# A hybrid decoder step on one core: when the pooling weights and the samples' caches are loaded

## The chip, the core and the metric

The kernel runs on one core of one Trainium2 chip. It is one launch that computes a whole layer for a prompt of 2048 tokens and for 8 samples of 8 tokens. The metric is the device time of that launch in microseconds; the smaller the better. The kernel is written with Tile, which turns the Python program into one instruction list per engine: it computes which instruction waits for which, and a list scheduler may move an instruction ahead of others of the same engine. Tiles come from fixed rings of slots, and the order in which slots are taken and given back is the order of the Python program.

## The reference

All weights are float32. `x` is the prompt or the samples, `D_MODEL` is 1024.

```python
h = rmsnorm(x, g_mix)
proj = h @ w_in                      # 512 q, 128 k, 128 v, 512 u
# 1a. window attention: 8 heads of 64, 2 kv heads, window 128, sink, ALiBi
#     prompt: blocks of 128;  samples: keys = cat(cache_win_k, k), values = cat(cache_win_v, v)
# 1b. pooling mixer on u: means over windows 2, 4, 8, 16 minus u, per channel group g
full = cat([u_prev, u])              # u_prev: state_pool for the samples, zeros for the prompt
y = einsum('blgc,gce->blge', d, w_pool) * pool_scale
x = x + cat([attn, y]) @ w_out
# 2. cross attention, 4 heads of 256, 256 memory tokens
q = rmsnorm(x, g_cross) @ w_cq;  mem_k = hm @ w_ck;  mem_v = hm @ w_cv   # hm = rmsnorm(mem)
x = x + softmax(q mem_k / 16) mem_v @ w_co
# 3. MLP
x = x + square(relu(rmsnorm(x, g_ffn) @ w_up)) @ w_down
# outputs also: the last 128 k and v rows and the last 15 u rows of prompt and samples, mem_k, mem_v
```

## The kernel before

**Arithmetic.** Every dense product is made of three TensorE matmuls: each operand is split into a high part (a float32r cast, `hi`) and the rest (`lo`), and hi·hi, hi·lo and lo·hi are added in PSUM (`mm3`, lines 122 to 124, and `dense`, lines 291 to 293). A weight chunk of 512 KB is loaded by SyncE (`SP`) into one of six float32 slots `f`, cast by ScalarE (line 143) and subtracted by VectorE (line 144) into two of twelve slots `w`; then the slot `f` is free again. `Stream` holds the list of all chunks in the order of their use and runs up to five chunks ahead, as long as enough slots are free (`pump`).

**Order of the program.** A prologue works on the prompt's memory; three superblocks of two token blocks each follow. In the prologue `mem_k` and `mem_v` are made first (chunks `wck`, `wcv`). Then comes the *query fold*, the loop over eight chunks `wcqt`: each gives two products of 128x512 that ScalarE copies from PSUM into a slot `f` (`put_fold`, line 342) and SP stores to the scratch tensor `a_s` (line 344). The *output fold* does the same with eight chunks `wco`, two at a time, into `b_s`. So in both folds the six slots `f` serve the loads and the stores. The norms of superblock 0's two blocks (`norm1`) run beside these folds.

**The lead of superblock 0.** The projection `h @ w_in` has ten chunks of 128 columns (`win`), each multiplied with block 0 (256 columns) and block 1 (320 columns, the last 64 of them the samples). A list `lead` says which products come before the attention starts: (chunk 0, block 0), (0, 1), (1, 0), (1, 1), (2, 0), (2, 1) and on to (5, 1). After each of the first four of them stands one `fold(g, wpr)`: the rows of `w_out` for pool group g (chunk `wop`) times the pooling weights, already scaled by `pool_scale` and split (`wpr`, one slot `w`), two products of 128x512 that are stored to `wo_s`. `prep_fold` makes `wpr`: it loads the constants `cst` (line 349) and the pooling weights `wpool` (line 351, 256 KB), and four ScalarE and four VectorE instructions scale and split them (lines 354, 355).

**What the samples need.** The samples' cached keys `ckz` (1 MB, line 534, into the tile X1 that held block 1's input), their cached values `cvz` (two loads of 512 KB into two slots `f`, line 522) and their pool state `spool` (line 517). `attn_sample` uses them after the lead: scores from `ckz` at line 785, values from `cvz` at line 824. The shifted caches are stored again: `out_wks` from `ckz` (line 561), `out_wvs` from `cvz` (line 778).

**Queues.** All these transfers are issued by SP, one after the other: while one of them waits for its slot, those behind it wait too.

Of the kernel before, what the change touches and what calls it, by code (L numbers as in the profile page):

```python
# [14 lines left out]
P = 128  # L15
# [41 lines left out]
def kernel(ctx: ExitStack, tc: tile.TileContext, io, nW=12, nF=6, nT=8):  # L57
    nc = tc.nc
# [288 lines left out]
    def prep_fold():  # L347
        wpr = WS.get()
        nc.sync.dma_start(cst[:], io["cst"])
        wp = FS.get()  # L350
        nc.sync.dma_start(wp[:, 0:512], io["wpool"])
        for g in range(4):
            c, sc = slice(P * g, P * g + P), vec[:, V_PSC + g:V_PSC + g + 1]
            nc.scalar.activation(wpr[:, c], wp[:, c], AF.Copy, scale=sc)
            nc.vector.scalar_tensor_tensor(wpr[:, 512 + P * g:640 + P * g], wp[:, c], sc, f32(wpr[:, c]), ALU.mult, ALU.subtract)
        FS.put(wp)
        return wpr

    def fold(g, wpr):
        th, tl = S.next(("wop", g))  # L360
        for eh in range(2):
            ps = MM.get()
            mm3(ps[:], [0], lambda k: wpr[:, P * g:P * g + P], lambda k: wpr[:, 512 + P * g:512 + P * g + P],
                lambda k: th[:, 512 * eh:512 * eh + 512], lambda k: tl[:, 512 * eh:512 * eh + 512])
            put_fold(ps[:], lambda o: [(wo_s[4 * eh:4 * eh + 4, :, P * g:P * g + P].rearrange("e p c -> p e c"),
                                        o[:, 0:512].rearrange("p (e c) -> p e c", c=P))])
            MM.put(ps)
        WS.put(th, tl)
        if g == 3:
            WS.put(wpr)  # L370

    def prologue():
        S.resW, S.resF = 1, 0
        mx = [XT[1][:, 0:1024], XT[1][:, 1024:2048]]
        mem = lambda k: mx[k // 4][:, 256 * (k % 4):256 * (k % 4 + 1)]
        warm = AUX.get()
        for _ in range(14):
            nc.tensor.matmul(warm[:, 0:P], ones[:], ident[:], start=True, stop=True)
        AUX.put(warm)
# [24 lines left out]
        pend, outs = [], []  # L404
        for name, dst in (("ck", io["mk"]), ("cv", io["mv"])):
            a = Act(256, GQ[len(outs)])
            outs.append(a)
            for c in range(8):
                th, tl = S.next((name, c))
                ps = MM.get()  # L410
                mm3(ps[:, 0:256], range(8), lambda k: w8(th)[:, k, :], lambda k: w8(tl)[:, k, :], hm.hi, hm.lo)
                WS.put(th, tl)
                pend.append((a, dst, c, ps))
                if name == "ck" and c == FINC:
                    nm.fin()
                if name == "cv" or c >= FINC:
                    while pend:
                        evac(*pend.pop(0))
                flush()
                if (name, c) == N1C:  # L420
                    norm1(blk[0][0], N1W)
        TS.put(nm.r)
        hm.free()
        mk, mv = outs
        norm1(blk[0][1], N1Q)
        for c in range(8):
            th, tl = S.next(("cq", c))
            for hf in range(2):
                ps = MM.get()
                for h2 in range(2):  # L430
                    ks = [(hf * 2 + h2) * 2, (hf * 2 + h2) * 2 + 1]
                    mm3(ps[:, 256 * h2:256 * h2 + 256], ks, lambda k: w8(th)[:, k, :], lambda k: w8(tl)[:, k, :], mk.hi, mk.lo)
                put_fold(ps[:], lambda o: [(a_s[hf, c // 2, :, 512 * (c % 2):512 * (c % 2) + 512], o[:, 0:512])])
                MM.put(ps)
            WS.put(th, tl)
            flush()
        mk.free()
        for h in range(4):
            w = [S.next(("co", 2 * h)), S.next(("co", 2 * h + 1))]
# [12 lines left out]
        mv.free()  # L452
# [46 lines left out]
    def superblock(s, blks, nxt):  # L499
        last = s == 2  # L500
        smp = blks[1] if s == 0 else None
# [12 lines left out]
        uext = X0[:, 0:4 * uw].rearrange("p (g t) -> p g t", t=uw)  # L514
        if smp:
            us = X0[:, 4 * uw:4 * uw + 736].rearrange("p (g b t) -> p g b t", g=4, t=23)
            nc.sync.dma_start(X0[:, 4 * uw:4 * uw + 736].rearrange("p (x t) -> p x t", t=23)[:, :, 0:15], io["spool"].rearrange("p (x t) -> p x t", t=15))
            ckz = X1[:, 0:2048].rearrange("p (b v s) -> p b v s", b=8, v=2)
            qz = [X1[:, 2048 + 544 * i:2048 + 544 * (i + 1)] for i in range(2)]
            cvs = [FS.get(), FS.get()]  # L520
            for i in range(2):
                nc.sync.dma_start(cvs[i][:, 0:1024], io["cvz"][:, 1024 * i:1024 * (i + 1)])
            cvz = [c[:, 0:1024].rearrange("p (b v s) -> p b v s", b=4, v=2) for c in cvs]
            smt = TS.get()
            kS = smt[:, 0:128].rearrange("p (v t) -> p v t", t=64)
            vS = smt[:, 128:384].rearrange("p (v t) -> p v t", t=P)
            nc.gpsimd.memset(smt[:, 0:384], 0.0)
            qf = TS.get()

        def in_evac(c, b, ps):  # L530
            bl = blks[b]
            n = bl.n
            if smp and (c, b) == (0, 0):
                nc.sync.dma_start(X1[:, 0:2048], io["ckz"])
                nc.gpsimd.memset(X1[:, 2048:3136], 0.0)
            if c == 0:
                for kv in range(2):
                    r = slice(64 * kv, 64 * kv + 64)
# [15 lines left out]
                if smp is bl:  # L554
                    t = TS.get()
                    nc.vector.tensor_copy(t[:, P:192], ps[:, bl.np:n])
                    nc.sync.dma_start(io["wks"][:, :, 120:128], t[:, P:192].rearrange("p (b t) -> p b t", t=8))
                    for kv in range(2):
                        r = slice(64 * kv, 64 * kv + 64)
                        nc.gpsimd.tensor_copy(kS[r, kv, :], t[r, P:192])  # L560
                        nc.sync.dma_start(io["wks"][r, :, 0:120], ckz[r, :, kv, 8:P])
                    TS.put(t)
            elif c == 1:
                nc.vector.tensor_copy(v32[:, bl.off:bl.off + n], ps[:, 0:n])
# [196 lines left out]

        def attn_sample():
            bl = smp
            LS = FS.get()
            t = st.get()
            dsm = cst[:, C_DS:C_DS + 384].rearrange("p (g s) -> p g s", s=192)
# [83 lines left out]
        def evac_in(c, b, ps):  # L850
# [2 lines left out]

        ug = dense([("in", s, c) for c in CIN], blks, hi1, lo1, evac_in, piece=2,
                   seq=lead + rest + [(c, b) for c in range(6, 10) for b in (0, 1)])
        if s == 0:
            wpr = prep_fold()
        while len(qdone) < len(lead):
            m = len(qdone)
            while len(qdone) == m:  # L860
                next(ug)
            if s == 0 and m < 4:
                fold(m, wpr)
        S.resW = RW

        def attn():
# [415 lines left out]
        down(7)  # L1282

    vcarry = [None]
    blk = [make_blks(s) for s in range(3)]
    prologue()
    for s in range(3):
# [132 lines left out]
```

## Time and profile before

| | us |
|---|---|
| median of 3 runs | 2657.72 (2656.19 to 2660.29) |
| the profiled execution, its own time | 2660.15 |
| span of the profiled execution | 2658.3 |
| TensorE (PE) busy | 2576.7 (97%) |
| VectorE (DVE) busy | 1298.3 (49%) |
| ScalarE (ACT) busy | 974.8 (37%) |
| GpSimd (POOL) busy | 658.9 (25%) |

The profile gives the busy time of each engine, the clock that TensorE was granted, and for each instruction its start, its duration and, where its engine stood idle before it, how long and which instruction ended that idle time (the releaser). PE is the row of matmuls, PEld that of weight loads. `f<-in_win` means that a slot `f` is written from the input tensor `win`. An SP row is the issue of a transfer and not the transfer; its duration is the time the issue took. Matmuls overlap, so the distance of two starts, not the duration, says how fast they follow each other.

### The profile page before, as it was taken

Reading aid. Unit: us, or ns where it says so; the run is one execution under the profiler, and the core shown is the slowest. Engines: PE = TensorE matmul, PEld = TensorE weight load, DVE = VectorE, ACT = ScalarE, POOL = GpSimd, SP = SyncE. Lnnn points to the kernel's source line nnn. Section 1 sums busy time; section 2 is a strip of 40 time slices with the busy share of each in tenths; the row PEclk is TensorE's granted clock in tenths of the full one; section 3 lists DMA queues with packets and bytes.
Section 4 is the critical chain, followed back from the end, with each engine's and each line's share of the span. In section 5 each row is a group of like instructions: output and inputs, shape, how many; then the busy total and the mean of one; then the engine's idle time right before and its main releaser. Section 6 shows DMA issues by size and latency. Waiting matters only on the chain.

```text
span 2658.3 us, 36411 instructions
## 1 busy us (share of the span) xinstructions
PE 2576.7 (97%) x14409; PEld 2407.6 (91%) x14409; DVE 1298.3 (49%) x2256; ACT 974.8 (37%) x1867; POOL 658.9 (25%) x695
## 2 busy tenths in 40 slices
PE   8789999999999999999999999999999999999998
PEld 8688858888879998899999999999979999999997
DVE  7547634644447856353333333689363633333333
ACT  6536424422334744333222222358243422222221
POOL 1205312311125343142111111525332411111111
PEclk9989999999999999999999999999999999999999
DMA  8842266223233041212111111222211111111101
GB/s 275 265 149 89 104 238 237 79 93 104 95 102 128 25 145 33 74 45 72 64 56 64 56 64 56 81 107 81 97 48 64 56 64 64 56 64 56 64 24 50
DMA packets 101823, 245.10 MB, mean 92 GB/s; under 512 B 21972, under 2 KB 41876, under 8 KB 101012
## 3 DMA queue, kind: packets, MB, share of 16 engines
q1 hardware_dynamic: 101652, 242.78, 26.9%
q8 instruction: 113, 1.85, 0.3%
q14 instruction: 58, 0.48, 0.1%
HBM read 219.79 MB, written 22.95 MB: 91 GB/s over the span
## 4 chain that ended last, share of the span: by engine, by line
PE 80%; DVE 8%; ACT 4%; POOL 3%; DMA 3%; issue 2%; SPq 0%; DVEq 0%; ACTq 0%; POOLq 0%
PE mm L124 13%; PE mm L122 13%; PE mm L123 13%; PE mm L292 13%; PE mm L293 12%; PE mm L291 12%; DVE t L243 3%; DVE w L144 1%; POOL t L217 1%; ACT w L143 1%; PE aux L699 1%; DVE acth L246 1%; POOL t L617 1%; ACT x L711 1%; PE aux L730 1%
## 5 line engine op out<-in xcount | busy, mean ns | idle before, releaser
L143 ACT CAST w<-f 128x1024 fp32r<-128x1024 f32 x311 | 325.9, 1050 | 693.3 <-PE mm L123 470.0
L144 DVE TENSOR_TENSOR w<-f,w 128x1024 fp32r<-128x1024 f32 x311 | 393.3, 1269 | 302.8 <-ACT w L143 298.4
L291 PE MATMUL mm<-acth,w 128*128 128x400 f32 (+3 forms) x1568 | 532.6, 340 | 6.6 <-ACT w L143 5.9
L293 PE MATMUL mm<-acth,w 128*128 128x400 f32 (+3 forms) x1568 | 529.4, 338 | 1.2 <-DVE w L144 1.2
L292 PE MATMUL mm<-acth,w 128*128 128x400 f32 (+3 forms) x1440 | 486.8, 338 | 6.1 <-DVE acth L246 5.4
L122 PE MATMUL mm<-actq,w 128*128 128x400 f32 (+2 forms) x1376 | 478.2, 348 | 1.1 <-ACT f L342 1.1
L124 PE MATMUL mm<-actq,w 128*128 128x400 f32 (+2 forms) x1376 | 478.7, 348 | 0.0
L123 PE MATMUL mm<-actq,w 128*128 128x400 f32 (+2 forms) x1248 | 433.5, 347 | 0.0
L1178 POOL TENSOR_TENSOR t<-t 128x400 f32<-128x400 f32 (+1 forms) x136 | 163.1, 1200 | 812.3 <-ACT t L1177 812.3
L291 PEld LDWEIGHTS mm<-acth,w 128*128 128x128 f32 x1568 | 298.1, 190 | 10.1 <-ACT w L143 6.8
L293 PEld LDWEIGHTS mm<-acth,w 128*128 128x128 f32 x1568 | 299.2, 191 | 1.7 <-DVE w L144 1.7
L1239 DVE TENSOR_TENSOR x<-mm,x 128x400 f32<-128x400 f32 (+1 forms) x272 | 152.9, 564 | 281.6 <-PE mm L124 278.6
L292 PEld LDWEIGHTS mm<-acth,w 128*128 128x128 f32 x1440 | 273.9, 190 | 11.2 <-DVE acth L246 7.3
L217 POOL TENSOR_TENSOR t<-t,t 128x384 f32<-128x384 f32 (+3 forms) x161 | 191.2, 1188 | 351.7 <-ACT t L216 348.3
L122 PEld LDWEIGHTS mm<-actq,w 128*128 128x128 f32 x1376 | 259.5, 189 | 11.7 <-ACT f L342 1.5
L124 PEld LDWEIGHTS mm<-actq,w 128*128 128x128 f32 x1376 | 260.8, 190 | 9.5
L291 PE MATMUL mm<-actq,w 128*128 128x384 f32 (+2 forms) x768 | 248.0, 323 | 0.8 <-DVE x L915 0.6
L293 PE MATMUL mm<-actq,w 128*128 128x384 f32 (+2 forms) x768 | 246.2, 321 | 2.0 <-DVE w L144 2.0
L292 PE MATMUL mm<-actq,w 128*128 128x384 f32 (+2 forms) x768 | 246.5, 321 | 0.0
L123 PEld LDWEIGHTS mm<-actq,w 128*128 128x128 f32 x1248 | 235.4, 189 | 9.9
L1180 DVE TENSOR_TENSOR actq<-t,actq 128x400 fp32r<-128x400 f32 (+1 forms) x120 | 71.1, 593 | 222.1 <-ACT actq L1179 222.0
L291 PEld LDWEIGHTS mm<-actq,w 128*128 128x128 f32 x768 | 145.6, 190 | 3.3 <-DVE x L915 0.9
(246 smaller groups left out, 3745.3 us busy)
## 6 DMA issues: line engine op xcount, KB each, us to landing
f<-in_wup SPq DMA_DIRECT2D x89, 512.0 KB, 3.2
f<-in_wdn SPq DMA_DIRECT2D x89, 512.0 KB, 3.2
f<-in_win SPq DMA_DIRECT2D x29, 512.0 KB, 3.2
f<-a_s SPq DMA_DIRECT2D x23, 512.0 KB, 3.8
f<-b_s SPq DMA_DIRECT2D x23, 512.0 KB, 4.2
f<-in_wco SPq DMA_DIRECT2D x16, 512.0 KB, 4.9
f<-in_cmk SPq DMA_DIRECT2D x16, 512.0 KB, 4.2
f<-in_cmv SPq DMA_DIRECT2D x16, 512.0 KB, 5.1
```

The lines of the kernel that those rows point to most:

```text
L122: nc.tensor.matmul(ps, Wh(k), Hh(k), start=first and i == 0, stop=False)
L123: nc.tensor.matmul(ps, Wh(k), Hl(k), start=False, stop=False)
L124: nc.tensor.matmul(ps, Wl(k), Hh(k), start=False, stop=final and i == last)
L143: nc.scalar.copy(th[:], r[:, 0:1024])
L144: eng.tensor_tensor(tl[:], r[:, 0:1024], f32(th[:]), ALU.subtract)
L217: self.add.tensor_tensor(self.acc[:, 0:n], self.acc[:, 0:n], t[:, 0:n], ALU.add)
L243: nc.vector.scalar_tensor_tensor(t[:, 0:n], self.x(k), vec[:, g + k:g + k + 1], self.r[:, 0:n], ALU.mult, ALU.mult)
L291: nc.tensor.matmul(ps[:, 0:n], w8(th)[:, k, :], hi(b, k), start=k == 0, stop=False)
L292: nc.tensor.matmul(ps[:, 0:n], w8(th)[:, k, :], lo(b, k), start=False, stop=False)
L293: nc.tensor.matmul(ps[:, 0:n], w8(tl)[:, k, :], hi(b, k), start=False, stop=k == 7)
L1178: nc.gpsimd.tensor_tensor(q, r, r, ALU.mult)
L1239: nc.vector.tensor_tensor(bl.x(m), ps[:, 0:n], bl.x(m), ALU.add)
```

## The change

`prep_fold` is called in the prologue, in the query fold before its fourth chunk, instead of in the superblock. The loads for the samples are written into the evacuations of projection chunks: `ckz` and the clearing of the rest of X1 at (2, 0) instead of (0, 0), `cvz` and `spool` at (4, 1) instead of at the superblock's start, and the stores of the shifted keys at the start of `attn_sample` instead of at (0, 1). The two slots `f` of `cvz` are taken only then.

```diff
@@ prologue
         for c in range(8):
+            if c == 3:
+                wpr.append(prep_fold())
             th, tl = S.next(("cq", c))
@@ superblock
-            nc.sync.dma_start(X0[:, 4 * uw:4 * uw + 736].rearrange(...)[:, :, 0:15], io["spool"].rearrange(...))
             ckz = X1[:, 0:2048].rearrange("p (b v s) -> p b v s", b=8, v=2)
...
-            cvs = [FS.get(), FS.get()]
-            for i in range(2):
-                nc.sync.dma_start(cvs[i][:, 0:1024], io["cvz"][:, 1024 * i:1024 * (i + 1)])
-            cvz = [c[:, 0:1024].rearrange("p (b v s) -> p b v s", b=4, v=2) for c in cvs]
+            cvs, cvz = [], []
@@ in_evac
-            if smp and (c, b) == (0, 0):
+            if smp and (c, b) == (2, 0):
                 nc.sync.dma_start(X1[:, 0:2048], io["ckz"])
                 nc.gpsimd.memset(X1[:, 2048:3136], 0.0)
+            if smp and (c, b) == (4, 1):
+                for i in range(2):
+                    cvs.append(FS.get())
+                    nc.sync.dma_start(cvs[i][:, 0:1024], io["cvz"][:, 1024 * i:1024 * (i + 1)])
+                    cvz.append(cvs[i][:, 0:1024].rearrange("p (b v s) -> p b v s", b=4, v=2))
+                nc.sync.dma_start(X0[:, 4 * uw:4 * uw + 736].rearrange(...)[:, :, 0:15], io["spool"].rearrange(...))
...
-                        nc.sync.dma_start(io["wks"][r, :, 0:120], ckz[r, :, kv, 8:P])
@@ attn_sample
             bl = smp
+            for kv in range(2):
+                r = slice(64 * kv, 64 * kv + 64)
+                nc.sync.dma_start(io["wks"][r, :, 0:120], ckz[r, :, kv, 8:P])
@@ superblock
-        if s == 0:
-            wpr = prep_fold()
...
-                fold(m, wpr)
+                fold(m, wpr[0])
@@ end
+    wpr = []
```

What the scheduler makes of it is seen in the order of SP's transfers. The slots f0 to f5 are called `f_79` to `f_84` there, and `x_94` is X1. In the query fold, between the last but one chunk `wcqt` and the third chunk `wco`, before:

```order
L142 DMA f_81<-in_wcqt 128x1024
L400 DMA out_mv<-t_92 128x256
L142 DMA f_84<-in_wcqt 128x1024
L344 DMA a_s<-f_82 128x512
L344 DMA a_s<-f_83 128x512
L344 DMA a_s<-f_79 128x512
L344 DMA a_s<-f_80 128x512
L142 DMA f_81<-in_wco 128x1024
...
L142 DMA f_84<-in_wco 128x1024
```

And now:

```order
L142 DMA f_81<-in_wcqt 128x1024
L400 DMA out_mv<-t_92 128x256
L351 DMA f_84<-in_wpool 128x512
L344 DMA a_s<-f_82 128x512
L344 DMA a_s<-f_83 128x512
L344 DMA a_s<-f_79 128x512
L344 DMA a_s<-f_80 128x512
L142 DMA f_79<-in_wcqt 128x1024
...
L142 DMA f_82<-in_wco 128x1024
...
L142 DMA f_79<-in_wco 128x1024
```

The pooling weights have the place of the last `wcqt` chunk, which comes after four stores and takes the slot that the third of them frees; the first `wco` chunk follows three stores later. `ckz`, which was issued ahead of the last store to `a_s`, is gone from there.

At the start of the lead, from the last store to `b_s` to the load of `win` chunk 1, SP's rows before:

```order
L344 DMA b_s<-f_79 128x4x128
L522 DMA f_82<-in_cvz 128x1024
L522 DMA f_81<-in_cvz 128x1024
L351 DMA f_83<-in_wpool 128x512
L561 DMA out_wks<-x_94 512x1x120
L557 DMA out_wks<-t_92 1024x1x8
L561 DMA out_wks<-x_94 512x1x120
L344 DMA wo_s<-f_84 128x4x128
L344 DMA wo_s<-f_79 128x4x128
L142 DMA f_83<-in_win 128x1024
```

And now, up to the load of `win` chunk 3:

```order
L344 DMA b_s<-f_80 128x4x128
L532 DMA x_94<-in_ckz 128x2048
L344 DMA wo_s<-f_82 128x4x128
L344 DMA wo_s<-f_83 128x4x128
L142 DMA f_84<-in_win 128x1024
L142 DMA f_79<-in_wop 128x1024
L561 DMA out_wks<-t_92 1024x1x8
L344 DMA wo_s<-f_80 128x4x128
L344 DMA wo_s<-f_82 128x4x128
L142 DMA f_83<-in_wop 128x1024
L142 DMA f_80<-in_win 128x1024
L142 DMA f_82<-in_win 128x1024
```

Between the last `b_s` store and the first `wo_s` store now stands one load, `ckz`, where six transfers stood. The two `cvz` loads stand behind the load of `win` chunk 6.

ScalarE's rows at the same place, from the cast of the second `wop` chunk to the cast of `win` chunk 1, before (`mm_95` to `mm_98` are the PSUM banks; lines 107 and 543 evacuate chunk 0):

```order
L543 CAST w_67<-mm_95 64x256
L543 CAST w_77<-mm_98 64x256
L107 CAST w_67<-mm_98 64x256
L543 CAST w_67<-mm_98 64x256
L354 ACTIVATE w_69<-f_83,vec 128x128 x4
L342 COPY f_84<-mm_96 128x512
L342 COPY f_79<-mm_97 128x512
L342 COPY f_79<-mm_95 128x512
L143 CAST w_70<-f_83 128x1024
```

And now:

```order
L143 CAST w_78<-f_82 128x1024
L107 CAST w_68<-mm_95 64x256
L342 COPY f_83<-mm_97 128x512
L342 COPY f_82<-mm_96 128x512
L547 CAST w_68<-mm_95 64x256
...
L342 COPY f_82<-mm_96 128x512
L547 CAST w_70<-mm_98 64x256
L143 CAST w_72<-f_84 128x1024
```

The four scalings of line 354 are gone from here (they stand in the query fold), and the copies of the first fold stand right behind the first evacuation of chunk 0. The second of these copies writes `f_82`, the slot from which the second `wop` chunk (`w_78`) is read.

More of the change, by code (lines that the diff above doesn't have):

```diff
@@ L516, in superblock @@
             us = X0[:, 4 * uw:4 * uw + 736].rearrange("p (g b t) -> p g b t", g=4, t=23)
-            nc.sync.dma_start(X0[:, 4 * uw:4 * uw + 736].rearrange("p (x t) -> p x t", t=23)[:, :, 0:15], io["spool"].rearrange("p (x t) -> p x t", t=15))
             ckz = X1[:, 0:2048].rearrange("p (b v s) -> p b v s", b=8, v=2)
             qz = [X1[:, 2048 + 544 * i:2048 + 544 * (i + 1)] for i in range(2)]
-            cvs = [FS.get(), FS.get()]
-            for i in range(2):
-                nc.sync.dma_start(cvs[i][:, 0:1024], io["cvz"][:, 1024 * i:1024 * (i + 1)])
-            cvz = [c[:, 0:1024].rearrange("p (b v s) -> p b v s", b=4, v=2) for c in cvs]
+            cvs, cvz = [], []
             smt = TS.get()
@@ L532, in in_evac @@
             n = bl.n
-            if smp and (c, b) == (0, 0):
+            if smp and (c, b) == (2, 0):
                 nc.sync.dma_start(X1[:, 0:2048], io["ckz"])
                 nc.gpsimd.memset(X1[:, 2048:3136], 0.0)
+            if smp and (c, b) == (4, 1):
[3 more added lines that the diff above has]
+                    cvz.append(cvs[i][:, 0:1024].rearrange("p (b v s) -> p b v s", b=4, v=2))
+                nc.sync.dma_start(X0[:, 4 * uw:4 * uw + 736].rearrange("p (x t) -> p x t", t=23)[:, :, 0:15], io["spool"].rearrange("p (x t) -> p x t", t=15))
             if c == 0:
```

## The prediction

> **What bounds the kernel now.** I read the page first: busy time of the engines and the slices by granted clock.
>
> ```profile
> span 2658.3 us, 36411 instructions
> PE 2576.7 (97%) x14409; PEld 2407.6 (91%) x14409; DVE 1298.3 (49%) x2256; ACT 974.8 (37%) x1867; POOL 658.9 (25%) x695
> PEclk9989999999999999999999999999999999999999
> ```
>
> TensorE is busy for 97% of the span, so only what keeps it waiting or slow can be gained: 82 us in all, and the third slice (133 to 199 us) is the only one whose clock digit is under 9. The edit acts from 60 us on, so next I cut that stretch into windows of 5 us (columns: PE, PEld, DVE, ACT, POOL busy, granted clock, DMA share, GB/s).
>
> ```profile
> 75.00:80.00 5.00, 5.00 (x40) 4.84 (x40) 1.63 (x2) 1.98 (x4) 1.43 (x1) 1.00 0.97 325
> 100.00:105.00 5.00, 3.31 (x13) 1.93 (x12) 0.00 (x0) 2.23 (x4) 0.00 (x0) 1.00 1.03 328
> 105.00:110.00 5.00, 4.37 (x12) 3.53 (x13) 2.45 (x2) 2.94 (x5) 0.00 (x0) 0.66 1.08 324
> 125.00:130.00 5.00, 0.00 (x0) 0.00 (x0) 2.77 (x7) 1.90 (x6) 1.60 (x6) 0.61 0.80 231
> 130.00:135.00 5.00, 3.66 (x9) 2.89 (x10) 1.23 (x4) 2.45 (x6) 0.00 (x0) 0.50 0.44 88
> 140.00:145.00 5.00, 3.79 (x16) 3.50 (x17) 2.45 (x2) 2.33 (x3) 0.00 (x0) 0.50 0.96 235
> 155.00:160.00 5.00, 4.23 (x18) 3.96 (x19) 2.45 (x2) 2.11 (x4) 0.00 (x0) 0.68 0.69 227
> ```
>
> Two things cost here: TensorE stands still, and after each stop it runs at about half clock for some microseconds. The timeline of PE gives the places (start, duration, and in brackets the idle time and its releaser).
>
> ```profile
> 88.67 0.50 PE L122 MATMUL mm<-w,actq 128*128 128x512 f32 x1
> ...
> 105.63 1.65 PE L122 MATMUL mm<-w,actq 128*128 128x512 f32 x3 [2.19 <-ACT w L143]
> ...
> 116.85 0.28 PE L291 MATMUL mm<-acth,w 128*128 128x256 f32 x1
> ...
> 119.72 0.31 PE L291 MATMUL mm<-acth,w 128*128 128x320 f32 x1
> ...
> 123.10 0.31 PE L293 MATMUL mm<-acth,w 128*128 128x320 f32 x1
> 131.34 0.80 PE L122 MATMUL mm<-w,w 128*128 128x512 f32 x1 [7.93 <-ACT w L354]
> ...
> 136.20 0.44 PE L124 MATMUL mm<-w,w 128*128 128x512 f32 x1
> 140.75 0.58 PE L291 MATMUL mm<-acth,w 128*128 128x256 f32 x1 [4.10 <-ACT w L143]
> ...
> 146.72 0.40 PE L122 MATMUL mm<-w,w 128*128 128x512 f32 x1
> ...
> 148.12 0.30 PE L291 MATMUL mm<-acth,w 128*128 128x320 f32 x1
> ...
> 155.07 0.42 PE L291 MATMUL mm<-acth,w 128*128 128x320 f32 x1 [1.78 <-ACT w L143]
> 156.33 0.42 PE L293 MATMUL mm<-acth,w 128*128 128x320 f32 x1 [0.70 <-DVE w L144]
> ```
>
> The output fold runs from 88.67 to 116.85 with one stop; the lead of the superblock starts at 116.85. Call that moment T. Chunk 0 takes 2.87 us with block 0 (116.85 to 119.72) and about 3.5 with block 1. Then TensorE waits 7.93 us for the scaled pooling weights, does two folds, waits 4.10 for chunk 1, and 1.78 and 0.70 for chunk 2. What these waits hang on is seen on SP, with the ScalarE and VectorE rows behind it.
>
> ```profile
> 66.59 0.34 SPq L142 DMA_DIRECT2D f<-in_wcqt  x1
> ...
> 74.05 0.33 SPq L142 DMA_DIRECT2D f<-in_wco  x1
> ...
> 93.00 0.40 SPq L534 DMA_DIRECT2D x<-in_ckz  x1
> 94.44 0.32 SPq L344 DMA_DIRECT2D a_s<-f  x1
> ...
> 100.28 0.84 SPq L142 DMA_DIRECT2D f<-in_wco  x2
> ...
> 122.58 2.02 SPq L522 DMA_DIRECT2D f<-in_cvz  x2
> 124.69 0.38 SPq L351 DMA_DIRECT2D f<-in_wpool  x1
> ...
> 133.69 1.66 SPq L344 DMA_DIRECT2D wo_s<-f  x2
> 135.45 0.45 SPq L142 DMA_DIRECT2D f<-in_win  x1
> ```
>
> ```profile
> 72.60 1.05 ACT L143 CAST w<-f 128x1024 fp32r<-128x1024 f32 x1
> ...
> 78.12 1.05 ACT L143 CAST w<-f 128x1024 fp32r<-128x1024 f32 x1 [3.02 <-DMA f<-in_wco]
> ...
> 130.89 1.28 ACT L354 ACTIVATE w<-f,vec 128x128 fp32r<-128x128 f32 x4 [2.74 <-DMA f<-in_wpool]
> 133.07 0.59 ACT L342 COPY f<-mm 128x512 f32<-128x512 f32 x1 [0.91 <-ACT w L354]
> ...
> 139.65 1.04 ACT L143 CAST w<-f 128x1024 fp32r<-128x1024 f32 x1 [1.29 <-DMA f<-in_win]
> ```
>
> ```profile
> 123.00 1.23 DVE L144 TENSOR_TENSOR w<-f,w 128x1024 fp32r<-128x1024 f32 x1 [2.25 <-ACT w L143]
> ...
> 131.32 1.23 DVE L355 SCALAR_TENSOR_TENSOR w<-f,vec,w 128x128 fp32r<-128x128 f32 x4 [2.46 <-ACT w L354]
> ```
>
> `wpool` is issued only at 124.69, behind the two `cvz` loads, which wait for slots until 122.58, and is scaled at 130.89. Chunk 1 is chained to it: its load (135.45) stands behind the two stores of the first fold (133.69), which wait for the copy at 133.07.
>
> **The change part by part.** *The pooling weights leave the lead.* Before, chunk 1 starts at 140.75, T + 23.9. Now the folds have their weights, and the chain to chunk 1 starts elsewhere: the second copy of the first fold goes into the slot of the second `wop` chunk, so it needs that chunk's split, which ended at 123.00 + 1.23 = 124.23, T + 7.4. From copy to chunk 1 the trace shows 133.07 to 140.75, 7.7 us (copy, two store issues, load, cast). So chunk 1 starts at T + 7.4 + 7.7 = T + 15.1, and this part gains 23.9 - 15.1 = **8.8 us**. TensorE has 2.87 + 3.5 + two folds of 1.4 (146.72 to 148.12 is one) = 9.2 us of work up to there: it still waits, for about 5.9 us in place of 12.
>
> *Behind chunk 1.* I leave its slow start as it is: 140.75 to 146.72 is 5.97 us for work that took 2.87 at full clock. The load of chunk 2 now stands three rows behind the second `wop` load and waits only for the store of the second fold, so the waits of 1.78 and 0.70 go, and with them the slow stretch after (4.23 us busy at 0.68: 1.4 us lost). **3.9 us.** What is late next is chunk 4, needed three products (9.8 us) after chunk 2: no wait.
>
> *The output fold.* `ckz` (1 MB) is issued at 93.00, and at the 328 GB/s of 100:105 takes 3.2 us of all DMA engines. The last store of the query fold behind it (94.44) and so the sixth `wco` load (100.28) come late: 2.19 us of wait, and 1.6 us at half clock after it (0.66 over 105:110 means some 3.3 us at half). Without it at most 3.8 us are gained. Against it stands the slot turn that `wpool` takes in the query fold: the last `wcqt` chunk, issued at 66.59, must now wait for a store to land (about 74), and each `wco` load comes some 5 us later, the first at 79 instead of 74.05. Its cast was done at 79.2 (78.12 + 1.05), for use at 88.67: 9.5 us in hand, so the first pair is in time. The later pairs have less. Ends: +3.8 if they hold, -5 if the whole delay comes through. I take **+1**, nearer to the upper end, since the sixth load, the one that made TensorE wait, no longer has `ckz` ahead of it.
>
> *The scaling itself.* ScalarE 1.28 us and VectorE 1.23 us now stand in the query fold, where the cast at 72.60 stood for a chunk needed at about 85.6 (88.67 less one chunk of 2.9 us): hidden by some 10 us of lead. Up to 1.3 us if that lead is used up by the slot turn. The slot `w` that it holds costs no prefetch: a chunk is fetched while three of twelve slots are free, so five chunks are held with eleven as with twelve.
>
> *`ckz` in the lead.* Issued at about T + 2 behind the last `b_s` store, its 3.2 us are over by T + 6, before chunk 1's load is issued (T + 9.7). Nothing; if it were still under way, 3.2 us. It writes X1, whose reader, the norm, ends before T. The clearing on POOL keeps its place among POOL's instructions.
>
> *`cvz`, `spool`, the stores.* Four stores of `out_wvs` and two of `out_wks` now stand among the later projection chunks. The values are first read here:
>
> ```profile
> 191.64 1.90 PE aux L824 x16
> ```
>
> In the new order `cvz` follows the stores of the fourth fold, at about T + 29, and lands some 5 us later, where this reader comes at T + 75 before and about T + 60 now: hidden by 25 us. SP waits there for the landing with two `win` loads behind, for chunks that are used after three more products of block 0: nothing, up to 2 us.
>
> **The sum:** 8.8 + 3.9 + 1 = 13.7 us. The profiled execution took 2660.15 us (2658.3 of span and 1.85 around it), so 2646.4; the median of the runs shown is 2.4 lower, so I predict 2644.0.
>
> *A rule of the skill.* The trace shows 3.3 us at half clock after a wait of 2.19 us, and 0.68 after one of 1.78. The Trainium skill (TensorE: Matmul & The Clock Gate, Part 1: The HAM clock gate) says that the clock halves only after an idle window of about 3.4 us. By that rule the 5.9 us still waited, if they fall into two parts of about 3, would leave chunk 1 at full clock, and an estimate by the page adds its 2.6 us to the gain. The sum here goes by the trace, in which shorter waits sufficed.
>
> **The rivals.** *A: the wait moves into the output fold.* The folds are near the DMA limit (0.97 at 325 GB/s in 75:80, over 1.0 later), and the query fold now loads `wpool` too. If the `wco` chunks come 5 us late throughout, T moves to about 122 and the 3.8 us aren't had: 8.8 + 3.9 - 5 = 7.7 us, 2650. Against it: 9.5 us in hand for the first pair.
>
> *B: nothing is gained.* Chunk 1 still stands behind two stores that need the second `wop` chunk's slot. If its split came at T + 14 instead of T + 7.4, and A's delay were added, 8.8 - 6.6 + 3.9 - 5 = 1.1 us would be left: 2657. For it: the DMA engines at 0.80 to 1.08 all through; against: `wop` and its place are the same as before.
>
> *C: slower.* The eight `wco` loads now rotate through two slots: load, cast and split of one chunk must end before the slot's next load. TensorE uses a chunk in 2.8 us. The rows of `wco` give about 3.6 us for each (74.05 to 78.12 for the landing, 1.05, 1.23 and some waiting, over two slots). With a load every 5.5 us, which needs landings of 8 us, the eighth chunk would be split 8 x 1.9 = 15 us after what is needed, and all 13 us above are lost: 2661 and more. It decides from landings of about 8 us on; the landings seen here are 4 to 6 (74.05 to 78.12, 94.44 to 100.28, 135.45 to 139.65).
>
> *D: all waits go.* The second `wop` chunk comes 5 us earlier relative to T (its load follows chunk 0's split, not T), chunk 1 hardly waits and stays warm: another 5.9 + 2.6, so 22 us, 2635.
>
> **How the numbers follow.** My forecast (10 to 20 us gained) gets 0.62, A (5.3 to 10) 0.18, D 0.08, B 0.07, C 0.05. A measurement of this kernel can tell about 0.2%, 5.3 us, from no change. Faster by more: 0.62 + 0.18 + 0.08 = 0.88; within: 0.07; slower: 0.05. The range from 2637 to 2652 takes in the forecast, A down to the price it names and a little more, and leaves out B, C and D, 2 in 10.
>
> **What the profile after would show.** Right: no wait on line 354; `wpool` issued before 70 us; between T and chunk 1 about 15 us, with a wait for ScalarE's cast of chunk 1 of some 4 us left; no wait at chunk 2; T between 113 and 117; `ckz` landed before chunk 1's load. Wrong: waits of several us at the second, third and fourth pair of `wco` chunks and T over 120 (A or C); chunk 1 at T + 20 or later (B); a stop in front of the samples' values at the line that was 824.

## The result and the profile after

The changed kernel takes 2643.09 us (median of 4 runs, 2639.01 to 2647.16), the kernel before 2657.77 beside it: ratio 0.9944, 95% interval 0.9926 to 0.9961. It is 14.7 us faster; 2644.0 was forecast, within 2637 to 2652.

The page of the kernel after, the lines that answer to those of before:

```profile
span 2637.2 us, 36413 instructions
PE 2565.5 (97%) x14409; PEld 2396.6 (91%) x14409; DVE 1300.1 (49%) x2256; ACT 974.2 (37%) x1867; POOL 658.7 (25%) x695
PEclk9999999999999999999999999999999999999999
```

The third slice no longer falls under 9. TensorE is busy for 11.2 us less although it does the same 14409 matmuls, so it spent less time at half clock; how much of that is this execution's luck is told below. The windows of 5 us over the stretch that the edit acts on, with the columns of before:

```profile
100.00:105.00 5.00, 3.62 (x15) 2.77 (x16) 2.45 (x2) 3.67 (x6) 0.00 (x0) 1.00 1.06 331
105.00:110.00 5.00, 5.00 (x23) 3.77 (x22) 1.22 (x1) 2.86 (x4) 0.00 (x0) 1.00 1.03 312
125.00:130.00 5.00, 1.69 (x6) 1.36 (x7) 2.79 (x5) 3.09 (x5) 1.01 (x4) 0.50 0.68 206
130.00:135.00 5.00, 5.00 (x32) 4.74 (x32) 1.79 (x3) 1.64 (x2) 0.00 (x0) 0.84 1.00 316
...
155.00:160.00 5.00, 5.00 (x41) 4.83 (x40) 2.58 (x11) 0.94 (x2) 0.00 (x0) 1.00 0.69 249
```

The output fold keeps its full clock (105 to 110: 1.00, before 0.66), and from 135 to 165 no window is slow (155 to 160: 1.00, before 0.68). One slow place is left, around 125 to 133. The timeline of PE after, at the places shown of before:

```profile
100.63 0.50 PE L122 MATMUL mm<-w,actq 128*128 128x512 f32 x1 [0.88 <-ACT w L143]
...
112.27 0.28 PE L291 MATMUL mm<-acth,w 128*128 128x256 f32 x1
...
123.06 0.50 PE L122 MATMUL mm<-w,w 128*128 128x512 f32 x1 [1.83 <-DVE w L548]
...
128.31 0.58 PE L291 MATMUL mm<-acth,w 128*128 128x256 f32 x1 [4.05 <-ACT w L143]
...
139.17 0.28 PE L291 MATMUL mm<-acth,w 128*128 128x256 f32 x1
```

T is 112.27 now (before 116.85). No wait names line 354 (`wpool` is issued at 65.61, in the rows below). Chunk 1 begins at 128.31, T + 16.0 (before T + 23.9), behind 4.05 us of waiting; chunk 2 at 139.17 without any. The rows of SP, ScalarE and VectorE that this hangs on:

```profile
65.61 0.34 SPq L351 DMA_DIRECT2D f<-in_wpool  x1
...
75.95 0.33 SPq L142 DMA_DIRECT2D f<-in_wco  x1
...
115.92 1.45 SPq L532 DMA_DIRECT2D x<-in_ckz  x1
120.47 0.91 SPq L344 DMA_DIRECT2D wo_s<-f  x2
121.44 0.54 SPq L142 DMA_DIRECT2D f<-in_win  x1
...
144.01 1.01 SPq L537 DMA_DIRECT2D f<-in_cvz  x2
```

```profile
119.86 0.59 ACT L342 COPY f<-mm 128x512 f32<-128x512 f32 x1 [0.55 <-DVE w L144]
...
127.22 1.04 ACT L143 CAST w<-f 128x1024 fp32r<-128x1024 f32 x1 [1.17 <-DMA f<-in_win]
```

```profile
118.60 1.23 DVE L144 TENSOR_TENSOR w<-f,w 128x1024 fp32r<-128x1024 f32 x1 [2.76 <-ACT w L143]
```

Behind the lead the first weight load of the samples' scores is a mark that all kernels share; I call it S. The rows of that line before, after, and in a second profile of the changed kernel (the run "again" below); the range in them runs from S:

```profile
L785 PEld LDWEIGHTS aux<-x x32: 186/192/192, 177.3 to 182.4; 128*128 128x128 f32 x32
```

```profile
L791 PEld LDWEIGHTS aux<-x x32: 186/192/192, 158.8 to 163.9; 128*128 128x128 f32 x32
```

```profile
L791 PEld LDWEIGHTS aux<-x x32: 186/192/192, 163.4 to 168.5; 128*128 128x128 f32 x32
```

From S to the end of the span it is 2481.0 us before, 2478.4 after, and 2482.9 in the second profile (span 2646.3): behind S no effect of the change is seen, and the profiles scatter there by some 2 us to either side. So the first profile, 21.1 us shorter in span than that of before, is a lucky one; up to S the two profiles of the changed kernel gain 18.5 and 13.9 us, and the medians say 14.7 and (again) 15.3.

The second profile also tells what the gain is made of. Over its whole span TensorE is busy for 2574.3 us, only 2.4 less than before. Between 60 us and S it stands still for 20.7 us before, 9.5 and 10.2 after, and is busy for 96.65 us before, 89.30 and 93.23 after. So in both profiles the larger part of the gain is time in which TensorE no longer waits (11.2 and 10.5 us), and the smaller part is busy time at a faster clock (some 7.4 and 3.4 us).

### The profile page after: what moved, and what is told of

It is laid out like the page before. It is cut to its first block, busy times and chain, and to the rows that moved or that the text cites. A ratio compares the mean times of both kernels' runs of the same rounds, so it can differ in the third digit from the quotient of the medians.

```text
span 2637.2 us, 36413 instructions
## 1 busy us (share of the span) xinstructions
PE 2565.5 (97%) x14409; PEld 2396.6 (91%) x14409; DVE 1300.1 (49%) x2256; ACT 974.2 (37%) x1867; POOL 658.7 (25%) x695
## 3 DMA queue, kind: packets, MB, share of 16 engines
q8 instruction: 113, 1.85, 0.3%
## 4 chain that ended last, share of the span: by engine, by line
PE 82%; DVE 8%; ACT 3%; POOL 3%; DMA 2%; issue 2%; SPq 0%; DVEq 0%; ACTq 0%; POOLq 0%
PE mm L122 13%; PE mm L124 13%; PE mm L123 13%; PE mm L292 13%; PE mm L293 13%; PE mm L291 13%; DVE t L243 2%; POOL t L217 1%; ACT w L143 1%; PE aux L702 1%; DVE w L144 1%; DVE acth L246 1%; POOL t L620 1%; PE aux L733 1%; ACT x L714 1%
## 5 line engine op out<-in xcount | busy, mean ns | idle before, releaser
L122 PEld LDWEIGHTS mm<-actq,w 128*128 128x128 f32 x1376 | 259.2, 188 | 10.7 <-ACT f L342 0.3
```

The costliest lines, as they stand in the source:

```text
L122: nc.tensor.matmul(ps, Wh(k), Hh(k), start=first and i == 0, stop=False)
```

## The experiments

Q is the start of the query fold (its first matmul). Per run: the profile's times from Q to T (both folds), from T to chunk 1 and from T to S (S is read to a tenth), and the median time of all runs. Every kernel was compared with the kernel before on the same chip.

| run | Q to T | T to chunk 1 | T to S | median us | ratio, 95% interval |
|---|---|---|---|---|---|
| before | 54.9 | 23.9 | 60.5 | 2657.8 | |
| the change | 50.9 | 16.0 | 46.5 | 2643.1 | 0.9944 (0.9926 to 0.9961) |
| again (e4) | 51.8 | 16.7 | 49.1 | 2644.3 | 0.9942 (0.9929 to 0.9954) |
| e1 pool weights only | 52.3 | 25.1 | 62.3 | 2658.8 | 0.9997 (0.9988 to 1.0006) |
| e2 caches only | 56.1 | 17.3 | 51.4 | 2652.1 | 0.9970 (0.9958 to 0.9982) |
| e5 = e1, key stores later | 52.5 | 18.7 | 55.9 | 2655.1 | 0.9986 (0.9977 to 0.9995) |
| e6 change, `cvz` early | 52.5 | 16.6 | 53.0 | 2653.8 | 0.9975 (0.9966 to 0.9984) |
| e9 change, slots of `cvz` held | 54.1 | 13.4 | 51.2 | 2650.8 | 0.9970 (0.9959 to 0.9981) |
| e7 own buffer for `wpool` | 54.0 | 17.6 | 49.3 | 2648.5 | 0.9957 (0.9945 to 0.9970) |
| e8 = e7, `ckz` later | 52.2 | 10.7 | 47.7 | 2645.2 | 0.9947 (0.9934 to 0.9959) |
| e3 folds later | 54.0 | 6.4 | 44.0 | 2642.1 | 0.9934 (0.9921 to 0.9946) |
| e10 = e3 + e8 | 55.5 | 6.4 | 43.9 | 2645.9 | 0.9952 (0.9938 to 0.9966) |

**Each half alone (e1, e2).** e1 keeps only the call of `prep_fold` in the prologue; e2 keeps everything else.

```diff
 # e1, against the change
-            if smp and (c, b) == (2, 0):
+            if smp and (c, b) == (0, 0):
...
-            cvs, cvz = [], []
+            cvs = [FS.get(), FS.get()]
...
 # e2, against the change
-            if c == 3:
-                wpr.append(prep_fold())
...
+        if s == 0:
+            wpr.append(prep_fold())
```

> Only the pooling weights move to the query fold; the loads for the samples stay where they were before. T is the start of chunk 0 of the lead, C1 that of chunk 1, L that of the samples' first score product; before they lie at T = 116.9, C1 = T + 23.9, L = T + 60.5, with the change at 112.3, T + 16.0, T + 46.5. Theory (the wait for the pooling weights is gone, but cvz now stands in front of the first fold's stores, holds two slots, and its second load waits for the second wop chunk's split at T + 6): no wait on the scaling; chunk 1's load goes out at about T + 14 in place of T + 9, C1 = T + 20, L = T + 52, so 5 to 7 us slower than with both moved, some 9 us faster than before. Rival 1 (the pooling weights alone were the stop): C1 = T + 16 and the same time as with both. Rival 2 (the loads for the samples were the stop, wherever the weights are): C1 = T + 22 to 24, no faster than before by more than 3 us.

> Only the samples' loads and stores move; the pooling weights are loaded and scaled at the superblock's start again. In SP's order the load of the weights follows the last b_s store and one store of the shifted keys, and chunk 1's load now stands right behind it, ahead of the folds' stores. Theory: the weights wait for a slot until the second wop chunk is split (T + 7), land at T + 11.5 and are scaled at T + 12.5, so the wait on the scaling stays at about 6 us (7.9 before), but chunk 1 is there when the folds end: no wait of 4 us; C1 = T + 18, L = T + 51, some 8 us faster than before and 5 to 7 slower than with both. Rival 1 (the pooling weights are all of it): within 3 us of before. Rival 2 (the samples' loads are all of it): the wait on the scaling under 2 us and the time of the full change.

e1 gained nothing: 0.9997. Its theory (chunk 1 at T + 20, some 9 us gained) missed, and its second rival's outcome, no gain, came. The wait for the pooling weights is gone there, and the whole of it stands in front of chunk 1. SP and PE of e1:

```profile
119.90 2.06 SPq L524 DMA_DIRECT2D f<-in_cvz  x2
122.01 0.42 SPq L536 DMA_DIRECT2D x<-in_ckz  x1
122.49 1.03 SPq L344 DMA_DIRECT2D wo_s<-f  x2
127.89 0.64 SPq L559 DMA_DIRECT2D out_wks<-t  x1
130.60 1.25 SPq L563 DMA_DIRECT2D out_wks<-x  x2
131.90 0.90 SPq L142 DMA_DIRECT2D f<-in_win  x1
```

```profile
138.75 0.58 PE L291 MATMUL mm<-acth,w 128*128 128x256 f32 x1 [13.15 <-ACT w L143]
```

Chunk 1's load is issued at 131.90 (T + 18.3; the theory had T + 14) although the first fold's stores, behind which it stands, went out at 122.49. Between them stand a store of this superblock's keys (`out_wks<-t`) and the two stores of the shifted keys (`out_wks<-x`), which read what `ckz` brings. e2 went as its theory had it: 7.5 us gained with the pooling weights still in the lead. PE of e2, the wait for the weights and the start of chunk 1:

```profile
129.50 0.80 PE L122 MATMUL mm<-w,w 128*128 128x512 f32 x1 [5.46 <-ACT w L354]
...
134.79 0.33 PE L291 MATMUL mm<-acth,w 128*128 128x256 f32 x1
```

The halves give 0.8 and 7.5 to 8.0 us, and together 15. But they don't stand in front of chunk 1 alike. With the pooling weights moved alone, chunk 1 stays late (T + 25.1): SP holds its load. With the caches moved alone, it starts at T + 17.3, within 1.3 us of the change, since its load now stands ahead of the fold's stores. What e2 lacks of the change lies elsewhere in its profile: 4 to 5 us in the folds from Q to T, where `ckz` is still loaded (at 92.48), and 2 to 4 us behind chunk 1.

**What held SP (e5).** e1 with one thing more, the two stores moved to `attn_sample`:

```diff
-                        nc.sync.dma_start(io["wks"][r, :, 0:120], ckz[r, :, kv, 8:P])
...
+            for kv in range(2):
+                r = slice(64 * kv, 64 * kv + 64)
+                nc.sync.dma_start(io["wks"][r, :, 0:120], ckz[r, :, kv, 8:P])
```

> The pool weights' fold preparation is moved as in the change, the samples' caches and pool state are loaded at the superblock's start as before, and of the change's second half only one thing is done: the two stores of the shifted keys (out_wks <- ckz), which wait for the key cache's landing, are issued in the samples' attention and no longer on SP ahead of chunk 1's load. With preparation alone (the first run) chunk 1 began 25.1 us after T. Theory (the stores held SP until the key cache had landed, and chunk 1's load stood behind them): chunk 1's load is issued about 4 us earlier against T, chunk 1 begins at T+19 to T+22, and the time is 3 to 6 us below the first run's, 2653 to 2656. Rival (what delays chunk 1 is the bytes of the value cache and the key cache in front of its load, whoever waits for them): chunk 1 begins within 1.5 us of T+25 and the time is within 1.5 us of the first run's 2658.8.

2655.13 us, 3.6 below e1, chunk 1 at T + 18.7: the place is the theory's, a little better. The time is in its range too, but by the two ratios the step is 2.9 us with an uncertainty of some 3.4, so time alone doesn't show it. SP and PE of e5:

```profile
121.31 0.42 SPq L536 DMA_DIRECT2D x<-in_ckz  x1
121.78 1.10 SPq L344 DMA_DIRECT2D wo_s<-f  x2
127.51 0.64 SPq L559 DMA_DIRECT2D out_wks<-t  x1
128.25 1.10 SPq L142 DMA_DIRECT2D f<-in_win  x1
```

```profile
133.76 0.58 PE L291 MATMUL mm<-acth,w 128*128 128x256 f32 x1 [8.53 <-ACT w L143]
```

`cvz` and `ckz` stand ahead of chunk 1's load as before, and it comes 3.65 us earlier on SP (5.1 us against T, which is 113.62 in e1 and 115.06 in e5). Another 6 us lie between the fold's stores (121.78) and a store of this superblock's keys (`out_wks<-t`, 127.51) that chunk 1's load also stands behind; in the change that store comes behind the load (126.78).

**What the value cache cost (e6, e9).** e6 puts the loads of `cvz` and their slots back at the superblock's start; e9 takes the slots there and loads later.

```diff
 # e6, against the change
-            cvs, cvz = [], []
+            cvs = [FS.get(), FS.get()]
+            for i in range(2):
+                nc.sync.dma_start(cvs[i][:, 0:1024], io["cvz"][:, 1024 * i:1024 * (i + 1)])
...
 # e9, against the change
-            cvs, cvz = [], []
+            cvs, cvz = [FS.get(), FS.get()], []
...
-                    cvs.append(FS.get())
```

> The full change, except that the value cache's two loads (1 MB) and their two slots stand at the superblock's start again, ahead of chunk 1's load on SP; nothing that stands behind them ahead of chunk 1's load waits for their landing. Theory (it is a wait on SP for a landing that costs, and a load in front of chunk 1's costs about its bytes): chunk 1 begins at T+16 to T+18.5, and the time is within 3 us of the change's 2643 to 2644. Rival (the megabyte and the two slots are what held chunk 1): chunk 1 begins at T+20 or later, and the time is 5 us or more above the change's, 2648 or more.

> The full change, except that the two slots of the value cache are taken at the superblock's start and held, while its two loads are issued later (now behind chunk 1's load and the first of the fold's weights, ahead of chunk 2's). The run with the loads at the superblock's start (e6) left chunk 1 where the change has it (T+16.6) and still lost 10 us: from chunk 1 to the first weight load of the samples' scores it took 36.4 us, the change 30.5 and 32.4, the kernel before 36.6. Theory (the slots: with two of six held through the lead, the fold's weights and chunk 2 pass through one slot, one after the other): chunk 1 begins by T+17, from chunk 1 to the samples' scores it takes 34.5 to 38 us, and the time is 2650 to 2655. Rival (the early megabyte, which took the bandwidth and the place on SP ahead of chunk 1's load): from chunk 1 to the samples' scores it takes 30 to 33 us and the time is within 3 us of the change's 2643 to 2644.

e6 was a miss for both theories as I had put them: chunk 1 came at T + 16.6, as in the change, and yet the time was 10 us above it. Most of the loss stands behind chunk 1 (36.4 us from there to S; the change 30.5 and 32.4). e9 told the two apart: chunk 1 even earlier (T + 13.4), 37.9 us from there to S, 2650.84 us: the held slots are the larger part, and the early transfer's part is not told from nothing. SP of e6, SP of e9, and PE of e9:

```profile
123.90 0.72 SPq L142 DMA_DIRECT2D f<-in_win  x1
128.09 0.34 SPq L142 DMA_DIRECT2D f<-in_wop  x1
...
133.77 0.33 SPq L142 DMA_DIRECT2D f<-in_wop  x1
...
141.35 0.82 SPq L142 DMA_DIRECT2D f<-in_win  x2
```

```profile
132.16 0.33 SPq L142 DMA_DIRECT2D f<-in_wop  x1
...
140.80 0.82 SPq L142 DMA_DIRECT2D f<-in_win  x2
```

```profile
128.70 0.58 PE L291 MATMUL mm<-acth,w 128*128 128x256 f32 x1 [3.25 <-ACT w L143]
...
145.26 0.58 PE L291 MATMUL mm<-acth,w 128*128 128x256 f32 x1 [2.89 <-ACT w L143]
```

With two of the six slots taken (and `v32` in a third), the last two `wop` chunks and chunk 2 go through one slot, one after the other (in both kernels' order of SP's transfers they all write the same slot): chunk 2 is loaded at about 141 instead of at 130.15 (the changed kernel's row of `in_win x2`), TensorE waits 2.89 us in e9 and 2.17 in e6, and the clock drops again (0.66 and 0.67 over 145 to 150).

The kernels from before to the change make a ladder, each step the difference of two ratios times 2659, in this order of the edits: `prep_fold` moved (e1) 0.8; the key stores off SP (e5) 2.9; `ckz` and `spool` later (e6) 2.9; the loads of `cvz` later (e9) 1.3; the two slots free (the change, e4) 7.4. Each ratio is uncertain by 2.4 to 3.3 us, and so each step behind the first by 3.4 to 4.4: only the last step is clear of its own uncertainty. It rests on the medians: e9's profile also took 2 to 3 us more from Q to T, where its transfers stand in the change's order, and that is scatter.

**The output fold (e7, e8).** Moving `prep_fold` changes the scheduler's order there too: with the slot turn of `wpool`, `ckz` leaves the output fold. e7 loads `wpool` into the idle buffer of the carried keys, and `ckz` returns; e8 holds it back by a copy of one column on POOL.

```diff
 # e7 and e8, against the change
-        wp = FS.get()
+        wp = f32(kcar[:])
...
-        FS.put(wp)
 # e8 alone
+                nc.gpsimd.tensor_copy(X1[:, 0:1], f32(kz[0][0][:, P:P + 1]))
                 nc.sync.dma_start(X1[:, 0:2048], io["ckz"])
```

> The full change, except that the pool weights (wpool) are loaded into the buffer of the carried keys, which is idle then, instead of taking one of the fold's slots; the key cache's load then stands in the output fold again, as in the kernel before. From Q to T the kernel before took 54.9 us and the change 50.9 and 51.8. Theory (the key cache's transfer among the weights of the output fold is what made that fold stop, and its leaving gave the 3 to 4 us that my forecast had put at 1): Q to T is 54 to 56 us and the time 2 to 4 us above the change's, 2645.5 to 2648. Rival (the slot turn that the pool weights take costs the output fold, the key cache nothing): Q to T is 51 us or less and the time up to 3 us below the change's.

> As the run before (pool weights in a buffer of their own), with the key cache's load held back behind a one-column copy on POOL that reads the first keys of chunk 0, so that it stands behind the output fold as in the change. It takes away both the slot turn and the key cache's transfer from that fold. If the key cache's transfer is the cost: Q to T is 50 to 51.5 us, about the change's, and 3 us or more below the run before. If the slot turn also costs something: Q to T is 49.5 us or less, 1.5 us or more below the change's. The time follows: 2641 to 2644, unless the held key cache load makes chunk 1's load late, which would show as chunk 1 later than T+17.

e7 takes 54.0 us from Q to T, as the theory had it, and 2648.5 us, half a microsecond above its range; e8 takes 52.2 and 2645.2, a little more than was expected and 3.3 us less than e7. That points to some 2 to 3 us for `ckz` among the fold's weights, but one pair doesn't show it: Q to T varies by itself. The profiles whose transfers on SP have the same order up to T (the change twice, e1, e5, e6, e9) took 50.9, 51.8, 52.3, 52.5, 52.5 and 54.1 us, the mean 52.4. All profiles together agree with it: the three kernels with `ckz` in the fold (before, e2, e7) took 54.9, 56.1 and 54.0, the nine profiles without it 50.9 to 55.5, on the mean 2.1 us less. The slot turn that I had priced at up to 5 us costs nothing that the profile shows: without it e8 is no faster than the change. The DMA engines have little left there: in the windows of 5 us from 100 to 110 of the changed kernel their share is 1.06 and 1.03 at 331 and 312 GB/s.

**A better version? (e3, e10, e4).** e3 moves the folds' products two lead products later, e10 adds e8's edits, e4 is the change unaltered.

```diff
 # e3 and e10, against the change
-            if s == 0 and c in (0, 1):
+            if s == 0 and c in (1, 2):
...
-            if s == 0 and m < 4:
-                fold(m, wpr[0])
+            if s == 0 and 2 <= m < 6:
+                fold(m - 2, wpr[0])
```

> The full change, and the four output-weight folds stand two products later in the lead (after chunk 1 with block 0, chunk 1 with block 1, chunk 2 with block 0, chunk 2 with block 1), with the wop chunks behind chunk 1 in the list of loads. Theory (what is left of the stop, 4.05 us before chunk 1 and 1.8 between the first two folds, is the chain from the second wop chunk over the first fold's stores to chunk 1's load): chunk 1 is loaded at about T - 2 and follows chunk 0 without a wait, C1 = T + 6.4; the two waits and 2 us at half clock go, L = T + 39 in place of T + 46.5, 6 to 8 us faster than the change. Rival (the stage is bound by the DMA engines, 0.9 to 1.08 busy, and only moves the wait on): waits of 4 us and more in front of the wop folds or chunk 2, L = T + 44 to 47, within 3 us of the change.

> The changed kernel once more, unaltered, to see what of its gain repeats. Its four runs lie between 2639.0 and 2647.2, its profiled run was the fastest, and 18.5 us of that run's 21.1 us were gained by L, the other 2.8 between L and the samples' memory loads, where the granted clock was 0.90 and 1.00 in place of 0.82 and 0.91. Theory (the lead's gain repeats, the rest is where stretches at half clock happen to fall): T within 1.5 us of 112.3, C1 - T within 1 us of 16.0, L within 2 us of 158.8; total 2639 to 2648, and differences of the total against the first run lie behind L in slices with another clock. Rival (the lead itself varies by 8 us from run to run): L at 161 to 167 and the same time from L to the end as in the first run.

> A candidate put together from the runs: the change, with the fold's products two lead products later and their weights behind chunk 1 in the list (as in e3, 2642.05), the pool weights in a buffer of their own and the key cache's load held behind POOL's copy (as in e8, 2645.2). From T to the samples' scores e3 took 44.0 us, e8 47.7, the change 46.5 and 49.1. If the freed slot matters in the lead: 42 to 44 us from T, and 2639 to 2642. If nothing is left to gain there, since the output fold's own waits and the granted clock decide: 44 to 46 us from T, and 2642 to 2645.

e4 repeated the time (2644.28) but not the lead: T at 114.31 and S at 163.4 lie 2.0 and 4.6 us later than in the first profile, more than the theory allowed, so executions of one kernel differ by some 5 us up to S.

With the folds later, chunk 1 has no wait at all (T + 6.4), and T to S falls to 44.0 and 43.9 us. The theory of e3 (6 to 8 us faster than the change) missed all the same, and its rival's outcome came, some 2 us: the stop moved on, though a smaller one, to 143.74 (1.85 us of waiting for a cast of weights, and a clock of 0.66 over 145 to 150). e3 is the fastest kernel of the study with 2642.05, but its interval overlaps that of e4, so it is not shown to beat the change. e10 was a miss: the freed slot did nothing in the lead, and in its profile it lost in the output fold, where the last pair of weights came late. Windows and PE row of e10:

```profile
108.00:110.80 2.80, 0.00 (x0) 0.00 (x0) 0.00 (x0) 1.05 (x2) 0.00 (x0) 1.00 0.94 313
110.80:114.00 3.20, 3.15 (x10) 2.39 (x11) 2.45 (x2) 1.76 (x3) 0.00 (x0) 0.71 0.94 277
```

```profile
110.85 0.73 PE L122 MATMUL mm<-w,actq 128*128 128x512 f32 x2 [2.98 <-ACT w L143]
```

The DMA engines carry 313 GB/s while TensorE waits. Whether e10's longer fold (55.5 us) is its own or the scatter of one execution, one profile can't tell; its median is 3.8 us above e3's.

## Why the prediction was right, point by point

- **Chunk 1 at T + 15.1, 8.8 us.** Measured T + 16.0 and 16.7: 7.9 and 7.2 us. The chain ran as written: split of the second `wop` chunk done at 118.60 + 1.23 = 119.83 (T + 7.6, forecast 7.4), copy at 119.86, load at 121.44, cast at 127.22, chunk 1 at 128.31. From copy to chunk 1 it took 8.45 us, not 7.7: from issue to cast 5.8 us instead of 4.2. The prediction put `ckz` in the lead at nothing, since it would be over before this load. It was not: issued at 115.92 (T + 3.7, forecast T + 2), it landed 7.0 us later, at about 122.9, when the load (121.44) was already under way. That this made the load's landing longer is likely and was not tested.
- **Whose gain this is** was put wrongly. I booked the 8.8 us under "the pooling weights leave the lead". That edit alone (e1) leaves chunk 1 at T + 25.1; the step reckons with a load that follows the fold's stores at once, and this holds only because the key stores were also moved off SP. The other half alone (e2) brings chunk 1 to T + 17.3 with the pooling weights still in the lead: 6.6 of the 7.2 to 7.9 us come without the edit that I booked them under. The diff has both, so the sum was right; the heading was not.
- **Chunk 2, 3.9 us.** From chunk 1 to S it took 36.6 us before, 30.5 and 32.4 after: 6.1 and 4.2. No wait is left at chunk 2. I argued from the rows on SP; the cause beneath them, two slots held by `cvz`, is what e9 shows. The second profile is near the forecast; what the first has beyond it I can't put on one row.
- **The output fold, +1.** Q to T fell by 4.0 and 3.1 us. Mis-sized: these two are near the upper end, 3.8, which I had reserved for no delay at all, and T came at 112.27 and 114.31 where I had 113 to 117; the mean of the six profiles with the same transfers, 52.4, gives 2.5. The profiles with and without `ckz` point to some 2 us from `ckz`, and the delay of the `wco` loads, 1.5 to 2.8 us on the first five, didn't come through. The first pair's load came at 75.95 (I had 79), and the waits of 0.88 and less took no clock (1.00 over 105 to 110).
- **The sum.** Up to S the second profile gives 3.1 + 7.2 + 4.2 less 0.5 (Q later) = 13.9 us beside the forecast 13.7; the first gives 18.5. The medians lie between. That the sum comes so close is in part luck: in the second profile chunk 1 gave 1.6 us less than its term, the folds 2.1 more, chunk 2 0.3 more.
- **The terms put at nothing.** The loads of `cvz` went out at 144.01 (T + 31.7, forecast T + 29) and landed 6.4 us later; the samples' values are first read at 173.10, without a wait there, as forecast. The term of `ckz` in the lead is answered above.
- **Rivals.** A: the output fold became shorter, not longer. B's outcome, nothing gained, is that of e1, though not through the second `wop` chunk but through the stores of keys on SP. C: no delay of the `wco` chunks built up; the waits in the fold stayed at 0.88 us and below. D, no wait at chunk 1, was reached by e3 and e8 and was worth little: in e3 T to S is 44.0 us against 46.5 and 49.1, while in e8, where only chunk 1 is early (T + 10.7), the folds and chunk 2 wait in its place (47.7).
- **The clock rule.** The waits left were 1.83 and 4.05 us, 5.9 in all as forecast, and chunk 1 started at half clock (0.50 over 125 to 130). In the second profile they were 1.83 and 3.50, and chunk 1 started at half clock too. The 2.6 us with which the prediction prices that slow start (beside the rule of the clock and in rival D) do not come out of its own rows: 5.97 less 2.87 is 3.1. By the rule of the Trainium skill (TensorE: Matmul & The Clock Gate, Part 1: The HAM clock gate) a halving needed one idle window of about 3.4 us; the 4.05 and the 3.50 agree with it. e8 does not: there the half clock followed a wait of 1.64 us. PE row and windows of e8:

```profile
138.22 0.58 PE L291 MATMUL mm<-acth,w 128*128 128x256 f32 x1 [1.64 <-ACT w L143]
```

```profile
133.00:138.00 5.00, 2.50 (x11) 1.28 (x9) 2.20 (x5) 1.85 (x3) 0.00 (x0) 0.99 0.89 289
138.00:143.00 5.00, 4.78 (x20) 4.45 (x21) 2.39 (x3) 2.16 (x3) 0.00 (x0) 0.50 1.00 289
```

TensorE was busy for only half of the 5 us ahead (2.50). The measurement decides: a wait shorter than that window can be enough; that the thin stretch ahead made the difference is likely and was not tested.

## What to carry to other kernels

When an edit has two halves, test each half and both, and look at what the moved wait is called now: here the half under which the gain had been booked gained nothing alone, since the wait only moved to the next instruction. Of every row that SP issues ahead of an urgent load ask not only how many bytes it moves but what it waits for: with the stores that waited for a landing out of the way, chunk 1 started 6.4 us earlier against T (e1 to e5), while its load still stood behind the megabyte of `cvz`. And count the slots that an early load holds, not only its transfer: two slots held through the lead were 7.4 us (uncertain by 4.4) of a gain of some 15.

## What the runs showed that I had not expected

The length of a wait alone doesn't foretell the clock. In the changed kernel waits up to 0.88 us in the output fold cost none (1.00 over 105 to 110), e10's 2.8 us without a matmul still show 1.00 and only the stretch behind them 0.71, and e8's 1.64 us ended in 0.50. The same wait of 2.0 us behind the lead, one row of before and one of after:

```profile
262.26 0.39 PE L293 MATMUL mm<-actq,w 128*128 128x256 f32 x1 [2.04 <-DVE w L144]
```

```profile
242.47 0.39 PE L293 MATMUL mm<-actq,w 128*128 128x256 f32 x1 [2.02 <-DVE w L144]
```

In windows of 20 us around them the granted clock is 0.91 before and 1.00 after, at the same place of the same work:

```profile
257.30:277.30 20.00, 17.96 (x122) 17.76 (x121) 10.26 (x16) 7.10 (x13) 7.19 (x11) 0.91 0.61 216
```

```profile
238.80:258.80 20.00, 17.98 (x134) 17.78 (x134) 11.71 (x16) 7.05 (x12) 7.39 (x10) 1.00 0.61 222
```

The other profiles show both outcomes at this place too, and not by the length of the wait: 0.91 behind waits of 2.01 to 2.03 us in e1, e6 and e7, 1.00 behind 2.02 to 2.04 in e2, e3 and e8. Both profiles of the changed kernel show 1.00 there. That such places are a part of why runs of one kernel spread over 8 us here (2640.07 to 2648.08 in e4) is likely and not shown. What decides whether such a wait slows the clock stays open.
